# Every fourth MLP weight chunk gets its low part from an accumulating DMA (first half) or from GpSimd (second half)

## The chip, the cores and the metric

One core of a Trainium2 chip runs the kernel in one launch. The metric is the device time of one execution in microseconds (us); lower is better. The engines are PE (TensorE, matmul), ACT (ScalarE), DVE (VectorE), POOL (GpSimd) and SP (SyncE, which here only issues DMAs); each works through its own queue in program order, and semaphores order them among each other. DMAs run on 16 DMA engines beside them.

## The reference

One decoder block on 256 tokens of 2048 features, float32: an mLSTM branch and an attention branch on a shared normalised input, merged by gates, then an MLP with 8192 hidden features and a gated embedding. The change touches the MLP alone:

```python
h = rmsnorm(x, mlp_norm[i])
x = x + jnp.square(jax.nn.relu(h @ w_ff1[i])) @ w_ff2[i]     # 2048 -> 8192 -> 2048
```

## The kernel before

Activations are kept as [feature, token]; a product takes weight tiles of 128 x 128 as the stationary operand and the activation of 256 tokens as the moving one. To get float32 accuracy from a faster pass, each operand is split into a high part H (rounded to float32r) and the exact rest L, and W.a = WH.aH + WH.aL + WL.aH. The activation's two parts lie side by side in one `blk` tile of 512 columns, so each weight tile needs two matmuls: its high part (`wh`) against all 512 columns, and its low part (`wl`) against the first 256.

All weights are packed in the order of their use into 518 chunks of 128 x 1024 (eight weight tiles, 512 KB), and two chunks make a pair, which is one DMA of 1 MB on SP's queue into a staging buffer `wst` (`STAGE` = 3 buffers, line 306). `plan()` lists the groups: after the projections, gates and the output product (226 chunks) come the MLP's 256, in four rounds of four groups `f1` and four groups `f2`, eight chunks each, then the embedding's products `pp` and `pg` (36 chunks). A column tile of f1 or f2 has 16 weight tiles, so every second chunk finishes one.

`run()` walks over the chunks with index i. At each it calls `prep(i + LOOK)`, `LOOK` = 3: ACT casts the staged chunk to `wh` (helper `copy`, line 170). Then the matmuls of chunk i are issued (`mm`, line 210). Then `side()` issues steps of side work (evacuation of finished tiles, splitting of new activations, norms) that a planner with estimated costs finds to fit beside the chunk, and `prep_rest(i + LOOK)`, there or right after: DVE subtracts `wl = wst - wh` (helper `tt`, line 178). `wh` and `wl` have `LOOK + 1` = 4 buffers each. When i + LOOK is odd, `prep_rest` also gives back the staging buffer of that pair and issues the load of the pair three further on (`self.dma(i // 2 + STAGE)`), which has to wait for the readers of the buffer.

A finished column tile of f1 is taken out of PSUM by ACT (`lo<-acc`, half of it) and DVE (`z<-acc,lo`), scaled, squared and split again into a `blk` tile, an operand of f2. A finished tile of f2 is added to x by DVE (`g<-g,acc`, twice). `z`, `lo`, `g`, `rb` and `blk` are these tiles' names in the profile; `load_x` (line 336) loads x, and later x again, into `g`.

Of the kernel before, what the change touches and what calls it, by code (L numbers as in the profile page):

```python
"""Hybrid mLSTM / attention block: one launch, activations kept as [feature, token].

Dense products run on the tensor engine as three float32r passes: every float32 operand is
split exactly into a rounded high part H (float32r) and the exact rest L, and
W.a = WH.aH + WH.aL + WL.aH.  The per-token factor of each RMS norm is applied to the product
instead of to its operand, so no product waits for the statistics.
"""
# [31 lines left out]

# columns of the packed per-feature parameters  # L40
C_G1, C_G2, C_G3, C_G4, C_CW, C_CB, C_MN, C_BIF = 0, 16, 32, 48, 64, 96, 104, 112
NCOL = 113
# columns of the constants
K_ID, K_CA, K_CB, K_FR, K_SG, NCON = 0, 128, 384, 768, 769, 770


def plan():
    """Order in which the weight chunks (128 x 1024) are used."""
    g = []
    for n in range(2):  # L50
        g.append(("av", n))
    g += [("mq", 0), ("mk", 0), ("gate", 0), ("mv", 0), ("mv", 1), ("mo", 0), ("mo", 1)]
    for n in range(2):
        g += [("aq", n), ("ak", n)]
    for n in range(4):
        g += [("gm", n), ("um", n)]
    for n in range(4):
        g += [("ga", n), ("ua", n)]
    for n in range(4):
        g.append(("wo", n))  # L60
    for j in range(4):
        g += [("f1", 4 * j + n) for n in range(4)] + [("f2", 4 * j + n) for n in range(4)]
    for n in range(4):
        g += [("pp", n), ("pg", n)]
    return g


def pack_weights(w_in, w_up_m, w_up_a, w_out, w_ff1, w_ff2, w_pg, w_pp):
    def rows(w):
        """Chunks of two k tiles with 512 columns (these weights are the moving operand)."""  # L70
        return w.reshape(-1, 2, 128, 512).transpose(0, 2, 1, 3).reshape(-1, 128, 1024)

    def tiles(w):
        """Chunks of eight 128 x 128 tiles, all k tiles of one column tile after another."""
        t = w.reshape(w.shape[0] // 128, 128, -1, 128).transpose(2, 0, 1, 3)
        return t.reshape(-1, 8, 128, 128).transpose(0, 2, 1, 3).reshape(-1, 128, 1024)

    out = []
    for name, n in plan():
        c = slice(512 * n, 512 * n + 512)  # L80
        if name == "gate":
            w = np.zeros((D, 128), np.float32)
            w[:, 0:4] = w_in[:, OFF["mi"]:OFF["mi"] + 4]
            w[:, 32:36] = w_in[:, OFF["mf"]:OFF["mf"] + 4]
        elif name in OFF:
            o = OFF[name] + 512 * n
            w = w_in[:, o:o + 512]
        elif name == "um":
            w = w_up_m[:, c]
        elif name == "ua":  # L90
            w = w_up_a[:, c]
        elif name == "wo":
            w = w_out[:, c]
        elif name == "f1":
            w = w_ff1[:, c]
        elif name == "f2":
            j, m = divmod(n, 4)
            w = w_ff2[2048 * j:2048 * j + 2048, 512 * m:512 * m + 512]
        elif name == "pg":
            w = w_pg[:, c]  # L100
        else:
            w = w_pp[:, c]
        out.append(rows(w) if name in ("av", "mv") else tiles(w))
    a = np.concatenate(out)
    return np.ascontiguousarray(a.reshape(-1, 2, 128, 1024).transpose(0, 2, 1, 3))


class Block:
# [21 lines left out]

# [1 line left out]
    @staticmethod  # L132
# [82 lines left out]

# [1 line left out]
    def spawn(self, gen, front=False):  # L217
# [16 lines left out]
    def side(self):  # L234
        """Runs the steps that fit beside the current chunk on the scalar and vector engines."""
        while True:
            lim = self.t["pe"] + BEYOND
            can = [t for t in self.tasks if t[1] <= self.now and t[2] <= lim]
            base = min(self.t["act"], self.t["dve"])
            best = min(can, key=lambda t: max(t[2], base)) if can else None  # L240
            if self.rest:
                r = max(self.t["dve"], self.ready(self.rest[2]))
                if not best or max(best[2], self.t["dve"]) >= r - 0.3:
                    self.prep_rest(self.now + LOOK)
                    continue
            if not best or max(self.t["act"], self.t["dve"]) >= lim:
                return
            self.advance(best)
# [14 lines left out]
    def settle(self, *aps):  # L263
        """Until products that read these would not hold up the tensor engine."""
        while self.ready(*aps) > self.t["pe"] and not self.forcing:
            yield 1
# [7 lines left out]
    def enter(self, kind, limit=2):  # L274
        """At most `limit` heads at a time, as many as there are buffers."""
        while self.inside.get(kind, 0) >= limit:
            yield 1
        self.inside[kind] = self.inside.get(kind, 0) + 1
# [6 lines left out]

# [1 line left out]
    def split(self, blk, src, gain=None):  # L287
        """blk = [H | L] of src (times a per-feature gain)."""
        if gain is None:
# [9 lines left out]
    def dma(self, p, load=True):  # L299
        """Loads two chunks."""  # L300
        if 2 * p >= self.nchunk:
# [6 lines left out]
    def load_w(self, p, a, b):  # L308
        """Part of a pair: its columns a to b."""
        t = self.stage[p].rearrange("p c n -> p (c n)")  # L310
        src = self.d["w"][p].rearrange("p c n -> p (c n)")
        self.nc.sync.dma_start(out=t[:, a:b], in_=src[:, a:b])  # L312

    def prep(self, i, parts=1):
# [8 lines left out]
        if parts == 1:  # L323
            self.copy(h, s)

    def prep_rest(self, i):
        if self.rest:
            l, s, h = self.rest
            self.tt(l, s, h.bitcast(F32), OP.subtract)
            self.rest = None  # L330
# [7 lines left out]
    def warm_up(self):  # L338
        """Keeps the tensor engine busy until the first operands are there, for its clock."""
        t = self.ps.tile([128, 512], F32, name="acc")  # L340
# [5 lines left out]

# [1 line left out]
    def square_in(self, key, src, keep=False):  # L348
# [13 lines left out]
    def rsqrt(self, y, v):  # L362
        """y = v ** -0.5, refined once; [128, few] columns."""
        s = self.tp.tile(list(v.shape), F32, name="rs_s")
# [6 lines left out]
    def spread(self, col):  # L371
        """out[p, t] = col[t] for every p: ones.T @ diag(col)."""
        rd = self.tp.tile([128, 2, 128], F32, name="rd", bufs=2)
# [44 lines left out]

# [1 line left out]
    def gather(self, dst, ps):  # L420
# [56 lines left out]

# [1 line left out]
    def col(self, c):  # L479
# [8 lines left out]
    def halves(self, blk, src, gain=None):  # L488
        """split(), with a step between the two parts."""
        if gain is None:  # L490
# [28 lines left out]
    def tables(self):  # L519
        """cos and signed sin of position * frequency, on the partitions of the rotated features."""  # L520
        yield 5
# [127 lines left out]
    def memory(self, h):  # L649
        """Head h of the mLSTM, in its quadratic form."""  # L650
        yield from self.wait("mv0" if h < 2 else "mv1")
# [52 lines left out]
    def read_out(self):  # L704
        """Normaliser and head norm of all heads, then the gated output."""
        yield from self.wait(*[f"mem{h}" for h in range(MH)])
# [34 lines left out]
    def attend(self, h):  # L741
        """Causal softmax attention of head h (the sequence is one block)."""
        n, m = divmod(h, 4)
# [85 lines left out]

# [1 line left out]
    def operand(self, name, n):  # L831
# [7 lines left out]
    @staticmethod  # L839
    def narrow(name, n):  # L840
        """Whether all three passes add up in the same columns, for a shorter way out."""
        return name == "pp" or (name, n) == ("pg", 3)

    def units(self, name, c):
        """(column tile, k tile) of each part of chunk c of a group."""
        if name in ("av", "mv"):
# [6 lines left out]
    def run(self):  # L853
# [3 lines left out]
        for name, n in groups:  # L857
            c = {"gate": 2, "um": 4, "ua": 4, "pp": 1}.get(name, 8)
            chunks += [(name, n, i, c) for i in range(c)]
        self.nchunk = len(chunks)  # L860
        assert self.nchunk == 2 * d["w"].shape[0]
        self.stage, self.w, self.val, self.acc, self.rb, self.rcol = {}, {}, {}, {}, {}, {}
# [108 lines left out]
    def finish(self):  # L971
        """The final norm."""
        self.forcing = True
# [61 lines left out]
```

## Time and profile before

| | us |
|---|---|
| median of 2 runs | 1502.16 (1501.99 to 1502.33) |
| profiled execution, first to last instruction (span) | 1499.9 |
| PE busy | 1484.6 |
| PE's weight loads busy (beside matmuls) | 1300.2 |
| DVE busy | 1041.5 |
| ACT busy | 760.2 |
| POOL busy | 0.2 |

The profile is of one execution; its times are from the start of the span. Busy times of different engines overlap. PE's matmuls are pipelined and their ends are modelled, so the starts of matmuls tell the pace. "PEld" is the loading of the stationary operand. "<-" in a row of an instruction has the tile written before it and the tiles read behind it.

### The profile page before, as it was taken

The numbers are of one execution on the slowest core, as the hardware profiler recorded it, in microseconds if no ns is written. First come the engines' busy times: TensorE is split into PE (matmuls) and PEld (weight loads), VectorE is DVE, ScalarE is ACT, GpSimd is POOL, SyncE is SP. The second block draws the span as 40 slices with busy tenths as digits, with TensorE's granted clock in tenths as the row PEclk, the third lists the DMA queues.
The fourth block names the chain that finished last, engine by engine and source line by source line (L and its number), as shares of the span: only waits on it lengthen the run. The fifth ranks groups of instructions, "written<-read, shape, count | busy, mean of one in ns | idle before, by whom it ended". The sixth has DMA issues, their size and how long they took to land.

```text
span 1499.9 us, 21023 instructions
## 1 busy us (share of the span) xinstructions
PE 1484.6 (99%) x8500; PEld 1300.2 (87%) x8500; DVE 1041.5 (69%) x1606; ACT 760.2 (51%) x1105; POOL 0.2 (0%) x4
## 2 busy tenths in 40 slices
PE   9999999999999999999999999999999999999996
PEld 7888888888888888888888888888888888888886
DVE  7685568987667677777765677666766567777775
ACT  7565544475445555455443445334543345455663
POOL 0000000000000000000000000000000000000000
PEclk9999999999999999999999999999999999999998
DMA  8554354544545555555555555555555545555451
GB/s 315 195 188 157 141 197 169 197 143 166 196 176 204 207 189 209 191 177 193 182 189 192 195 184 184 195 196 186 182 202 195 196 174 193 197 196 184 182 194 59
DMA packets 41472, 279.97 MB, mean 187 GB/s; under 512 B 4736, under 2 KB 5536, under 8 KB 8608
## 3 DMA queue, kind: packets, MB, share of 16 engines
q1 hardware_dynamic: 41232, 278.58, 51.6%
q8 instruction: 66, 1.08, 0.3%
q14 instruction: 30, 0.25, 0.0%
q10 hardware_dynamic: 144, 0.06, 0.0%
HBM read 276.52 MB, written 2.10 MB: 186 GB/s over the span
## 4 chain that ended last, share of the span: by engine, by line
PE 99%; DVE 0%; DMA 0%; ACT 0%; SPq 0%; issue 0%; DVEq 0%
PE acc L210 98%; DMA wst<-w 0%; DVE g L178 0%; PE acc L214 0%; ACT L811 0%; SPq L336 0%; ACT wh L170 0%; DVE rd L178 0%; DVE z L178 0%; ACT sq L166 0%; SPq L312 0%; ACT z L166 0%; DVEq L1030 0%; ACT rs_s L166 0%; DVE r L205 0%
## 5 line engine op out<-in xcount | busy, mean ns | idle before, releaser
L210 PE MATMUL acc<-blk,wh 128*128 128x512 f32 (+1 forms) x3984 | 1362.4, 389 | 0.0
L210 PE MATMUL acc<-blk,wl 128*128 128x256 f32 x3888 | 1088.5, 280 | 0.0
L210 PEld LDWEIGHTS acc<-blk,wh 128*128 128x128 f32 x3984 | 740.4, 188 | 162.5
L178 DVE TENSOR_TENSOR wl<-wst,wh 128x1024 fp32r<-128x1024 f32 (+1 forms) x521 | 633.6, 1217 | 230.1 <-ACT wh L170 216.8
L170 ACT CAST wh<-wst 128x1024 fp32r<-128x1024 f32 (+1 forms) x521 | 545.4, 1047 | 374.1 <-PE acc L210 316.9
L210 PEld LDWEIGHTS acc<-blk,wl 128*128 128x128 f32 x3888 | 734.4, 189 | 0.4
L170 ACT COPY lo<-acc 128x256 f32<-128x256 f32 x173 | 64.6, 373 | 242.8 <-PE acc L210 242.8
L178 DVE TENSOR_TENSOR g<-g,acc 128x256 f32<-128x256 f32 (+2 forms) x166 | 72.1, 437 | 49.2 <-PE acc L210 46.5
L178 DVE TENSOR_TENSOR z<-acc,lo 128x256 f32<-128x256 f32 x76 | 32.3, 425 | 65.9 <-ACT lo L170 65.9
L178 DVE TENSOR_TENSOR g<-acc,lo 128x256 f32<-128x256 f32 x96 | 40.4, 421 | 46.4 <-ACT lo L170 46.2
L210 PE MATMUL acc<-wh,blk 128*128 128x512 f32 x256 | 70.9, 393 | 1.6 <-ACT wh L170 1.6
L210 PEld LDWEIGHTS acc<-wh,blk 128*128 128x128 f32 x256 | 47.3, 188 | 12.1 <-ACT wh L170 2.6
L210 PE MATMUL acc<-wl,blk 128*128 128x512 f32 x128 | 40.9, 390 | 0.0
L170 ACT CAST blk<-z 128x256 fp32r<-128x256 f32 x64 | 26.1, 408 | 29.1 <-DVE z L189 29.1
L178 DVE TENSOR_TENSOR z<-z,rb 128x256 f32<-128x256 f32 x76 | 32.3, 425 | 3.1 <-ACT rb L170 0.6
L166 ACT ACTIVATE sq<-g 128x256 f32<-128x256 f32 x64 | 25.7, 409 | 10.1 <-DVE g L178 9.5
L210 PEld LDWEIGHTS acc<-wl,blk 128*128 128x128 f32 x128 | 24.0, 188 | 5.5 <-DVE wl L178 0.4
L189 DVE SCALAR_TENSOR_TENSOR z<-z 128x256 f32<-128x256 f32 x64 | 27.2, 424 | 2.2
L178 DVE TENSOR_TENSOR nacc<-nacc,sq 128x256 f32<-128x256 f32 x59 | 24.8, 421 | 3.8 <-ACT sq L166 2.9
L178 DVE TENSOR_TENSOR blk<-z,blk 128x256 fp32r<-128x256 f32 x64 | 26.8, 418 | 0.0
L166 ACT ACTIVATE blk<-g,cols 128x256 fp32r<-128x256 f32 x48 | 23.9, 509 | 2.5 <-DMA cols<-cols 1.4
L178 DVE TENSOR_TENSOR g<-g,rb 128x256 f32<-128x256 f32 (+1 forms) x46 | 24.2, 528 | 1.3
(115 smaller groups left out, 360.0 us busy)
## 6 DMA issues: line engine op xcount, KB each, us to landing
wst<-w SPq DMA_DIRECT2D x256, 1024.0 KB, 4.8
wst<-w SPq DMA_DIRECT2D x4, 512.0 KB, 6.8
g<-x SPq DMA_DIRECT2D x4, 512.0 KB, 5.8
g<-x SPq DMA_DIRECT2D x6, 256.0 KB, 6.9
out_dram<-g SPq DMA_DIRECT2D x3, 512.0 KB, 2.8
wst<-w SPq DMA_DIRECT2D x4, 256.0 KB, 5.6
g<-x SPq DMA_DIRECT2D x4, 128.0 KB, 5.2
con<-con SPq DMA_DIRECT2D x1, 385.0 KB, 8.2
```

The source lines that it names most:

```text
L166: self.nc.scalar.activation(out, in_, func, **kw)
L170: self.nc.scalar.copy(out, in_)
L178: self.nc.vector.tensor_tensor(out, a, b, op=op)
L189: self.nc.vector.scalar_tensor_tensor(out, a, s, b, op0, op1)
L210: self.nc.tensor.matmul(out, lhsT=lhsT, rhs=rhs, start=start, stop=stop)
```

## The change

Of the MLP's 256 chunks those with i % 4 == 1 get their low part in another way; all others as before.

- First half (the first 128 chunks of the MLP): after the cast to `wh`, ACT writes -1 times the staged chunk, rounded to float32r, into `wl`; a DMA issued by POOL then adds the chunk from DRAM, where it lies in float32, into `wl`. The weight is read from DRAM a second time for this.
- Second half: POOL does the subtraction that DVE did.

The helpers that charge the planner are not called for the DMA and for POOL's subtraction; for ACT's copy they are. The rest of the diff takes out comments and docstrings (left out here).

```diff
@@ def prep(self, i, parts=1):
         if parts == 1:
             self.copy(h, s)
+            if self.way(i) == "dma":
+                self.act(l, s, AF.Copy, scale=-1.0)
+
+    def way(self, i):
+        j = i - self.first["f1"]
+        if i % 4 != 1 or not 0 <= j < 256:
+            return "dve"
+        return "dma" if j < 128 else "pool"
 
     def prep_rest(self, i):
         if self.rest:
             l, s, h = self.rest
-            self.tt(l, s, h.bitcast(F32), OP.subtract)
+            way = self.way(i)
+            if way == "dma":
+                self.nc.gpsimd.dma_start(out=l, in_=self.d["w"][i // 2][:, i % 2], accum_op=OP.add)
+            elif way == "pool":
+                self.nc.gpsimd.tensor_tensor(l, s, h.bitcast(F32), op=OP.subtract)
+            else:
+                self.tt(l, s, h.bitcast(F32), OP.subtract)
             self.rest = None
             if i % 2:
                 del self.stage[i // 2]
                 self.dma(i // 2 + STAGE)
@@ def run(self):
+        self.first = {}
+        for i, (name, n, c, nch) in enumerate(chunks):
+            self.first.setdefault(name, i)
```

## Rows read from the trace of the kernel before

**Rows 1.** Page: busy us (share of span) and instructions of each engine.

```profile
PE 1484.6 (99%) x8500; PEld 1300.2 (87%) x8500; DVE 1041.5 (69%) x1606; ACT 760.2 (51%) x1105; POOL 0.2 (0%) x4
```

**Rows 2.** Page: chain that ended last, share of the span by engine.

```profile
PE 99%; DVE 0%; DMA 0%; ACT 0%; SPq 0%; issue 0%; DVEq 0%
```

**Rows 3.** PE's waits, whole span: us in total, times, longest us.

```profile
PE acc L210 <- ACT sq L166: 2.4, 1, 2.4
PE acc L210 <- DVE rd L178: 1.7, 1, 1.7
```

**Rows 4.** Stretches: us, busy us (instructions) by engine, granted clock, DMA share, GB/s.

```profile
673.00:1027.00 354.00, 354.00 (x2045) 312.13 (x2044) 232.69 (x326) 157.07 (x194) 0.00 (x0) 1.00 0.53 189
1027.00:1381.00 354.00, 354.00 (x2045) 312.14 (x2044) 243.35 (x352) 168.16 (x224) 0.00 (x0) 1.00 0.53 190
```

**Rows 5.** Tiles wl and wh, 673:1381: duration ns min/median/max, first and last start.

```profile
L210 PEld LDWEIGHTS acc<-blk,wl x2040: 187/189/192, 673.1 to 1380.9; 128*128 128x128 f32 x186
L178 DVE TENSOR_TENSOR wl<-wst,wh x256: 1216/1226/1226, 672.2 to 1380.4; 128x1024 fp32r<-128x1024 f32 x128
...
L170 ACT CAST wh<-wst x255: 1048/1053/1056, 673.9 to 1379.3; 128x1024 fp32r<-128x1024 f32 x128
```

**Rows 6.** Timeline of PE: start us, us, line, what; three chunks begin in it.

```profile
760.73 0.39 PE L210 MATMUL acc<-blk,wh 128*128 128x512 f32 x1
760.96 0.28 PE L210 MATMUL acc<-blk,wl 128*128 128x256 f32 x1
761.08 0.39 PE L210 MATMUL acc<-blk,wh 128*128 128x512 f32 x1
...
763.50 0.39 PE L210 MATMUL acc<-blk,wh 128*128 128x512 f32 x1
...
766.28 0.39 PE L210 MATMUL acc<-blk,wh 128*128 128x512 f32 x1
```

**Rows 7.** Timeline of ACT, DVE and SP there; in brackets idle before, and its releaser.

```profile
760.93 0.37 ACT L170 COPY lo<-acc 128x256 f32<-128x256 f32 x1 [1.80 <-PE acc L210]
761.20 1.05 ACT L170 CAST wh<-wst 128x1024 fp32r<-128x1024 f32 x1
762.60 1.22 DVE L178 TENSOR_TENSOR wl<-wst,wh 128x1024 fp32r<-128x1024 f32 x1
762.72 0.41 ACT L170 CAST blk<-z 128x256 fp32r<-128x256 f32 x1 [0.46 <-DVE z L189]
763.85 10.73 SPq L306 DMA_DIRECT2D wst<-w  x3
766.36 1.05 ACT L170 CAST wh<-wst 128x1024 fp32r<-128x1024 f32 x1 [1.68 <-PE acc L210]
```

**Rows 8.** Page: DMA issues with KB each and median us from issue to landing.

```profile
wst<-w SPq DMA_DIRECT2D x256, 1024.0 KB, 4.8
...
g<-x SPq DMA_DIRECT2D x4, 512.0 KB, 5.8
...
out_dram<-g SPq DMA_DIRECT2D x3, 512.0 KB, 2.8
```

**Rows 9.** Tile wst, whole span: landing of its loads.

```profile
DMA to landing us min/median/max: 4.2/4.8/8.9
```

**Rows 10.** Stretches of one weight load, issued at 763.85; last columns DMA share, GB/s.

```profile
763.85:764.80 0.95, 0.95 (x8) 0.83 (x7) 0.39 (x2) 0.83 (x1) 0.00 (x0) 1.00 0.00 0
764.80:765.80 1.00, 1.00 (x7) 0.89 (x6) 1.00 (x1) 0.00 (x0) 0.00 (x0) 1.00 0.60 164
765.80:766.80 1.00, 1.00 (x7) 0.90 (x6) 0.46 (x2) 0.44 (x1) 0.00 (x0) 1.00 0.98 418
766.80:767.80 1.00, 1.00 (x7) 0.88 (x7) 0.87 (x3) 0.61 (x1) 0.00 (x0) 1.00 1.00 426
767.80:768.70 0.90, 0.90 (x7) 0.78 (x6) 0.87 (x1) 0.00 (x0) 0.00 (x0) 1.00 0.12 46
```

**Rows 11.** Timeline of POOL, one of its four instructions.

```profile
0.30 0.10 POOL L1025 MEMSET const-bfloat16-1.0<- 128x1 bf16 x1
```

## The prediction

> **What bounds the kernel now.** I read the page's busy line and chain first, then PE's waits, then the two halves of the MLP as stretches of their own, and last a timeline of a few chunks. The busy line and the chain say the same: PE is busy 99% of the span and the chain that ends last is PE for 99% [rows 1, 2]. The longest of PE's four kinds of named waits are 2.4 and 1.7 us in the whole span [rows 3]. A busy PE need not be a PE at its peak, so I look at the pace: in the MLP the matmuls start in a fixed rhythm, one pair (512 columns with the high part, 256 with the low part) every 0.35 us, one chunk of eight pairs every 2.77 us (763.50 - 760.73; 766.28 is again 2.78 on) [rows 6]. The MLP takes from about 673 to 1381 us, 256 x 2.77 = 709 us, and PE is busy in 354.00 of 354.00 us of each half, at a granted clock of 1.00, the 2.4 GHz level [rows 4]. There is no wait in this stretch for the change to remove. DVE (66% and 69% there) and ACT (44% and 48%) both have room, POOL has done nothing, and the DMA engines are 53% busy [rows 4].
>
> So the question is only whether the new way of making the low part is ready when PE wants it.
>
> **The window.** Chunk i+3 is prepared while PE works on chunk i. Of the four buffers for low parts the one it takes was read last by chunk i-1, so the work starts when chunk i-1 ends and must be done when chunk i+3 starts: three chunks, 8.3 us, whatever happened earlier. No lead can be built up, so a part that is late is late anew each time. In an f1 stretch ACT first copies the finished column tile (760.93), then casts the high part (761.20, 1.05 us) [rows 7]. The chunk began at 760.73, so chunk i+3 begins at 760.73 + 3 x 2.77 = 769.04; its first matmul with the low part starts 0.23 later, as 760.96 after 760.73 [rows 6], and the weight load ahead of that takes 0.19 [rows 5]: the low part is wanted at 769.08. In f2 there is no copy before the cast: chunk start 766.28, cast 766.36, wanted at 774.63 [rows 6, 7]. Today DVE's subtraction is done by 763.82 in the first case (762.60 + 1.22), five microseconds early.
>
> **The change, part by part.**
>
> *Chunks.* f1 and f2 hold 256 chunks and begin at chunk 226; those with i % 4 == 1 are 64, 32 in each half. Of the first 32, half are prepared behind an f1 chunk and half behind an f2 chunk.
>
> *Removed:* 64 subtractions on DVE at 1.226 us [rows 5], 78 us of busy time, all of it hidden under PE. Worth 0.
>
> *Added on ACT, first half:* 32 copies of 128x1024 scaled by -1. The nearest row is the cast of the same shape, 1.05 us [rows 5]; 34 us more on an engine that is busy 157 of 354 us [rows 4]. They stand right behind the cast on ACT. Queued behind is the cast of the hidden tile (762.72 in the f1 example [rows 7]), which would start at about 763.3; its user is an f2 chunk, at the earliest one and a half chunks on. 0 by itself, but it delays the start of the DMA.
>
> *Added on POOL, first half:* 32 accumulating DMAs of 512 KB, issued when ACT's copy is done: 761.20 + 2 x 1.05 = 763.30 in f1, 766.36 + 2.10 = 768.46 in f2. Window to landing: 769.08 - 763.30 = 5.8 us, and 774.63 - 768.46 = 6.2 us. PE's first weight load of a low part waits for it, all matmuls behind it in order, and ACT's next cast behind those: each late microsecond goes to the end of the kernel in full.
>
> How long does such a DMA take? The trace has none. From below: 512 KB out of the core at the end, with the engines free, land in 2.8 us [rows 8]; then it is hidden. The nearest row in size and surroundings is the four loads of 512 KB of x, made beside the stream of weights: 5.8 us [rows 8]. Beside a weight load this one stands as well, and by more than chance: i is odd in every such chunk, so the same line of the program that issues it then issues the load of the next pair, which waits for the same ACT copy (the last reader of the staging buffer). SP's load has no traffic for 0.95 us after its issue at 763.85, and then fills the 16 engines, 0.98 to 1.00 busy at 418 to 426 GB/s, for two of the four microseconds that it takes [rows 10]. Both want the same engines in the same microseconds. An addition into memory has also to fetch the old values: another 512 KB, at 426 GB/s 1.23 us. POOL has to write the descriptors, which SP's queue does not need; for that I put 0.3 us, a third of SP's own 0.95. Sum: 5.8 + 1.23 + 0.3 = 7.3 us. From above: the slowest of all weight loads, in the crowd at the start, landed after 8.9 us [rows 9], with 0.3 for POOL 9.2.
>
> The nearest row decides, with the second fetch. Late by 7.3 - 5.8 = 1.5 us behind f1 and 7.3 - 6.2 = 1.1 us behind f2: 16 x 1.5 + 16 x 1.1 = 41.6 us. At 9.2 us it is 16 x 3.4 + 16 x 3.0 = 102 us, at 2.8 us nothing.
>
> Without the second fetch the DMA would land after 6.1 us, 0.3 us late in f1 only, 5 us in all. The Trainium skill, "Collectives: The Full Stack", section "The bandwidth ceiling: the fold count and why AG ≠ RS ≠ AR", bears on this: it says that an adding transfer is slower not by the addition but by its two source reads, which share one read ring, so that it runs at half the rate of a copy. No run here shows it yet; with it the sum is 41.6 us, without it 5 us.
>
> *Added on POOL, second half:* 32 subtractions of 128x1024. POOL's only rows are one-column memsets of 0.10 us [rows 11], of no use. From below DVE's 1.226 us. From above there is the window: the high part is there at 762.25 in f1, wanted at 769.08, so anything under 6.8 us, five and a half times DVE's time, costs PE nothing. I take 0. What hides it is the three-chunk window; if POOL needed 8 us it would be 1.2 us each, 38 us in all.
>
> *Moved:* the next pair's load follows ACT or POOL instead of DVE. Now it is issued 3.1 us into the chunk (763.85 - 760.73 [rows 6, 7, 10]), lands 4.8 us later [rows 8] at 7.9, and is wanted five chunks after the chunk's start, at 13.9: 6 us to spare, enough for the 1.2 to 2.5 us that sharing engines with the accumulating DMA may take or for a POOL that is slower than DVE. 0. Traffic: 16.8 MB more to read from memory and as much to fetch in the core, in 354 us; the stretch moves 189 GB/s, 67 MB, at 53% [rows 4], so 0.53 x (1 + 33.6 / 67) = 0.80 at most on average: the engines don't become the bound. The planner no longer charges DVE for these subtractions and may place side steps earlier; DVE has a third of its time free. 0.
>
> **Sum:** span 1499.9 + 41.6 = 1541.5 us, and 2.3 us around it (1502.16 median of the runs less 1499.9): **1544 us**, 2.8% slower.
>
> **The rivals.**
>
> *The DMA is hidden, or nearly* (not slower): it lands within 6.9 us, at most 0.9 us late on the mean window of 6.0. Then 0 to 30 us, 1502 to 1532 us. The point from which it decides is a landing at 5.8 to 6.2 us. For it: 512 KB alone in 2.8 us, and the x loads at just 5.8. Against it: twice the bytes to read and a weight load released in the same moment. Chance 0.38.
>
> *The DMA is very late:* over 9.2 us, because the engines add slowly or POOL needs microseconds to write its descriptors. At 12 us it would be 16 x 6.2 + 16 x 5.8 = 192 us, 1694 us. No row speaks for it, none excludes it. Chance 0.15.
>
> *POOL and DVE hold each other off in the second half.* DVE is busy 243 of 354 us [rows 4], 7.6 us in four chunks of 11.1; less one subtraction 6.4, leaving 4.7 us. If DVE stood still whenever POOL reads, a POOL subtraction of over 4.7 us would make DVE the bound; at 6 us, 1.3 us in each of 32, 42 us, with the DMA hidden 1544 us as well but lost in the other half. Chance 0.03. The Trainium skill, "SBUF — State Buffer", section "Who interferes with whom", says that a DVE instruction with two SBUF inputs is blocked by a GpSimd instruction that reads SBUF; and "GPSIMD Engine Reference", section "Elementwise — side-by-side cycle accounting", gives 4497 ns for 2048 columns on GpSimd, by which I estimate 2.25 us here, well under that point. No row shows POOL's price yet.
>
> *Faster by over 2%:* would need 30 us out of a stretch in which PE never waits. Chance 0.01.
>
> **How the numbers follow.** My forecast, a landing between 6.9 and 9.2 us and so a loss of 30 to 102 us (1532 to 1604 us), gets 0.43; the others as above. 2% is 30 us, about what a measurement of this kernel can tell from no change. Faster 0.01; within 2% 0.38; slower 0.43 + 0.15 + 0.03 = 0.61. The range takes in the hidden case and my own up to 9.2 us: 1500 to 1604 us, leaving out the very late one and the odd ones. My forecast's own range is 1532 to 1604.
>
> **What would show each step.** Right: PE waits, about 32 of them, for a DMA into wl between 673 and about 1070 us, 1 to 2 us each, and none behind it; a DMA row wl<-w of 32 issues with a median near 7.3 us; an ACT row of 32 scaled copies near 1.05 us; a POOL row of 32 subtractions under 6.8 us; PE's pace of 2.77 us for a chunk unchanged between the waits. Wrong: a landing under 6 us and no waits (hidden), a POOL queue that issues much later than ACT's copy ends, PE waits for POOL or DVE in the second half, or a PE pace that differs without waits, for which nothing in the trace of before prepares me.

## The result and the profile after

| | before | after |
|---|---|---|
| median of the runs, us | 1502.16 | 1576.43 (1573.18 to 1579.68, 2 runs) |
| profiled execution, span, us | 1499.9 | 1577.9 |

The changed kernel is slower: ratio 1.0495, 95% interval 1.0444 to 1.0547. The prediction was 1544 us, 2.8% slower, with a range to 1604; the sign and the place were right, the size was 74 us instead of 42.

The page's engine line and the chain that ended last, of the changed kernel, answer [rows 1, 2]:

```profile
PE 1509.9 (96%) x8500; PEld 1305.8 (83%) x8500; DVE 1008.4 (64%) x1542; ACT 788.4 (50%) x1137; POOL 108.1 (7%) x68
...
PE 80%; DMA 16%; ACT 1%; DVE 1%; issue 0%; SPq 0%; DVEq 0%; ACTq 0%
```

A chain that was PE for 99% now passes through a DMA for 16%. PE's waits in the whole span (us in total, times, longest us), against [rows 3], name it:

```profile
PE acc L210 <- DMA wl<-w: 53.5, 32, 2.1
```

and the weight loads' own:

```profile
PEld acc L210 <- DMA wl<-w: 63.8, 32, 2.4
```

All 32 accumulating DMAs are late, by about 2 us, and nothing else is new: no wait for POOL's 32 subtractions. The instructions that write wl (duration ns min/median/max, first and last start), against [rows 5]:

```profile
L166 ACT ACTIVATE wl<-wst x32: 1048/1058/1065, 672.1 to 1086.2; 128x1024 fp32r<-128x1024 f32 x32
L340 POOL DMA_DIRECT2D wl<-w x32: 862/862/1016, 673.5 to 1087.6; - x32
L342 POOL TENSOR_TENSOR wl<-wst,wh x32: 2391/2506/2619, 1099.4 to 1449.9; 128x1024 fp32r<-128x1024 f32 x32
```

The loss by halves is read from ACT's casts into `wh`, one for each chunk. The MLP's first starts at 671.13 us before and at 671.14 after. These are the casts 128 and 256 chunks later, before:

```profile
1027.05 1.06 ACT L170 CAST wh<-wst 128x1024 fp32r<-128x1024 f32 x1 [1.72 <-PE acc L210]
1382.09 1.06 ACT L170 CAST wh<-wst 128x1024 fp32r<-128x1024 f32 x1 [1.74 <-PE acc L210]
```

and after:

```profile
1098.23 1.05 ACT L170 CAST wh<-wst 128x1024 fp32r<-128x1024 f32 x1 [3.49 <-PE acc L210]
1460.04 1.05 ACT L170 CAST wh<-wst 128x1024 fp32r<-128x1024 f32 x1 [1.78 <-PE acc L210]
```

The first half took 427.1 us for 355.9, 71.2 more; the second 361.8 for 355.0, 6.8 more. Together 78, the difference of the spans.

The second half has no new wait. It is slower because PE's pace is: in a stretch of 100 us of the changed kernel (columns as in [rows 4]) there are 568 matmuls, 284 pairs, of 0.353 us; 579 in the same stretch of e2 below, 0.3467 us as before.

```profile
1100.00:1200.00 100.00, 100.00 (x568) 86.67 (x567) 72.15 (x93) 47.69 (x68) 22.64 (x9) 1.00 0.53 188
```

The DMA table's new row beside [rows 8], KB each and median us to landing (SP's loads of 1 MB stay at 4.8):

```profile
wl<-w POOLq DMA_DIRECT2D x32, 512.0 KB, 7.9
```

One of the 32, in order of time. First the issue: ACT, SP and POOL in the timeline; SP's load and POOL's DMA both wait for ACT's copy, which ends at 766.68.

```profile
765.62 1.06 ACT L166 ACTIVATE wl<-wst 128x1024 fp32r<-128x1024 f32 x1
766.58 0.39 ACT L170 CAST blk<-z 128x256 fp32r<-128x256 f32 x1
766.70 0.33 SPq L306 DMA_DIRECT2D wst<-w  x1
766.97 0.86 POOL L340 DMA_DIRECT2D wl<-w  x1 [12.63 <-ACT blk L170]
```

Then the DMA engines from POOL's issue on (last two columns: their share, GB/s). Up to 771.37 they move 246 to 295 GB/s, which is SP's load of 1 MB: 0.42 + 0.59 MB in the two long stretches. Only then comes a stretch in which they are full (1.03) and yet move 201 GB/s, with PE busy half of it: the addition, 4.4 us after its issue.

```profile
766.97:767.67 0.70, 0.70 (x7) 0.62 (x6) 0.43 (x1) 0.57 (x2) 0.70 (x1) 1.00 0.12 12
767.67:769.37 1.70, 1.70 (x12) 1.50 (x11) 1.19 (x1) 0.48 (x1) 0.17 (x1) 1.00 0.83 246
769.37:771.37 2.00, 2.00 (x14) 1.75 (x13) 0.98 (x4) 1.32 (x2) 0.00 (x0) 1.00 0.87 295
771.37:774.47 3.10, 1.54 (x9) 1.10 (x7) 2.54 (x4) 1.45 (x2) 0.00 (x0) 1.00 1.03 201
```

And PE: the matmul with the low part starts 2.27 us after the one ahead of it instead of 0.23, and what follows runs at half the clock for a while.

```profile
772.52 0.39 PE L210 MATMUL acc<-blk,wh 128*128 128x512 f32 x1
774.79 0.38 PE L210 MATMUL acc<-blk,wl 128*128 128x256 f32 x1 [1.88 <-DMA wl<-w]
775.01 0.55 PE L210 MATMUL acc<-blk,wh 128*128 128x512 f32 x1
...
776.22 0.63 PE L210 MATMUL acc<-blk,wh 128*128 128x512 f32 x1
776.64 0.41 PE L210 MATMUL acc<-blk,wl 128*128 128x256 f32 x1
```

The granted clock of that stretch is 0.50, the 1.2 GHz level, after a wait of 2 us:

```profile
775.10:778.50 3.40, 3.40 (x12) 2.88 (x11) 0.00 (x0) 0.00 (x0) 0.00 (x0) 0.50 0.54 227
```

So three things are to be explained: why each DMA lands after 7.9 us, what the falls of the clock add, and why PE keeps a slower pace where it waits for nothing.

### The profile page after: what moved, and what is told of

Same layout as the page of the kernel before. It is cut to its first block, busy times and chain, and to the rows that moved or that the text cites. A ratio compares the mean times of both kernels' runs of the same rounds, so it can differ in the third digit from the quotient of the medians.

```text
span 1577.9 us, 21147 instructions
## 1 busy us (share of the span) xinstructions
PE 1509.9 (96%) x8500; PEld 1305.8 (83%) x8500; DVE 1008.4 (64%) x1542; ACT 788.4 (50%) x1137; POOL 108.1 (7%) x68
## 4 chain that ended last, share of the span: by engine, by line
PE 80%; DMA 16%; ACT 1%; DVE 1%; issue 0%; SPq 0%; DVEq 0%; ACTq 0%
PE acc L210 80%; DMA wl<-w 16%; DVE g L178 1%; ACT wl L166 1%; DMA wst<-w 0%; PE acc L214 0%; ACT wh L170 0%; ACT L826 0%; SPq L351 0%; DVE rd L178 0%; DVE z L178 0%; ACT sq L166 0%; SPq L312 0%; ACT z L166 0%; DVEq L1048 0%
## 5 line engine op out<-in xcount | busy, mean ns | idle before, releaser
L210 PE MATMUL acc<-blk,wh 128*128 128x512 f32 (+1 forms) x3984 | 1379.2, 393 | 0.0
L210 PEld LDWEIGHTS acc<-blk,wl 128*128 128x128 f32 x3888 | 736.5, 189 | 64.2 <-DMA wl<-w 63.8
L178 DVE TENSOR_TENSOR wl<-wst,wh 128x1024 fp32r<-128x1024 f32 (+1 forms) x457 | 554.9, 1215 | 249.1 <-ACT wh L170 239.4
L340 POOL DMA_DIRECT2D wl<-w x32 | 27.8, 868 | 1060.2 <-ACT wl L166 855.5
L342 POOL TENSOR_TENSOR wl<-wst,wh 128x1024 fp32r<-128x1024 f32 x32 | 80.2, 2505 | 283.7 <-ACT wh L170 283.7
L178 DVE TENSOR_TENSOR blk<-z,blk 128x256 fp32r<-128x256 f32 x64 | 53.4, 834 | 21.3 <-ACT blk L170 21.3
L189 DVE SCALAR_TENSOR_TENSOR blk<-g,cols,blk 128x256 fp32r<-128x256 f32 x48 | 35.3, 743 | 9.1 <-ACT blk L166 9.1
L166 ACT ACTIVATE wl<-wst 128x1024 fp32r<-128x1024 f32 x32 | 33.8, 1057 | 0.0
```

The costliest lines, as they stand in the source:

```text
L166: self.nc.scalar.activation(out, in_, func, **kw)
L178: self.nc.vector.tensor_tensor(out, a, b, op=op)
L189: self.nc.vector.scalar_tensor_tensor(out, a, s, b, op0, op1)
L210: self.nc.tensor.matmul(out, lhsT=lhsT, rhs=rhs, start=start, stop=stop)
L340: self.nc.gpsimd.dma_start(out=l, in_=self.d["w"][i // 2][:, i % 2], accum_op=OP.add)
L342: self.nc.gpsimd.tensor_tensor(l, s, h.bitcast(F32), op=OP.subtract)
```

## The experiments

The theories on the DMA: **A**, its data queue behind SP's load, which the same ACT copy releases and which is issued 0.27 us ahead; **B**, the start by POOL takes 4.4 us by itself. On the pace: **1**, it is a state that a break in PE's sequence can set and that lasts until the next; **2**, POOL's work slows PE. In all kernels with the DMA alone (e1, e3 to e6, e9) the second half is done by DVE as before; each of these six was run once. Runs of the kernel before beside them lie between 1501.3 and 1502.4 us.

**e1: the accumulating DMAs alone.**

```diff
-        return "dma" if j < 128 else "pool"
+        return "dma" if j < 128 else "dve"
```

> Only the accumulating DMAs of the first half; the second half is done by DVE as before. In the changed kernel the first half cost 71.2 us and the second 6.8 us, the latter without any wait, as a slower pace of PE (284 pairs of matmuls in 100 us where there were 289 or 290). Theory 1 (the pace is a state that PE falls into after a stall and keeps): second half again some 7 us slower, 1576 us in all. Theory 2 (POOL's work slows PE): second half as before, 1571 us. Both: 32 waits for the DMA, 59 us.

Measured 1587.3 us (one run; span 1585.5). The second half is slow without POOL, 284 pairs in 100 us:

```profile
1200.00:1300.00 100.00, 100.00 (x569) 86.67 (x568) 60.15 (x77) 38.72 (x41) 0.00 (x0) 1.00 0.53 192
```

Theory 2 falls. The total is 11 us above what I expected: 32 waits again, of 66.9 us on PE's weight loads, and a mean clock of 0.988 where the changed kernel had 0.993. This run had seven falls of the clock after waits, the changed kernel's profiled one three. In each of these 3.4 us a pair takes some 0.64 us instead of 0.35, so about 1.5 us are lost, and four more make 6. The waits are 3.1 us longer (66.9 for 63.8), and the pace between them is some 2 us better than in the changed kernel. Together that is about the 7.6 between the two spans.

**e2: POOL's subtractions alone.**

```diff
-        return "dma" if j < 128 else "pool"
+        return "dve" if j < 128 else "pool"
```

> Only the subtractions on POOL in the second half; the first half as before. Theory 1 (pace is a state after a stall): no stalls, pace stays at 289 to 290 pairs in 100 us, 1502 us. Theory 2 (POOL's work slows PE): 284 pairs in 100 us in the second half, 1509 us. Rival from the prediction (POOL and DVE hold each other off): PE waits for wl from DVE or POOL.

Measured 1501.95 us, ratio 1.0001 (0.9992 to 1.0011). The pace is the quick one, with POOL at work:

```profile
1100.00:1200.00 100.00, 100.00 (x579) 88.15 (x578) 57.59 (x75) 41.41 (x46) 22.12 (x9) 1.00 0.53 196
```

POOL's half of the change costs nothing. DVE and POOL do hold each other off, though: DVE's subtraction that splits the hidden activations, 418 ns in every case before, now takes up to five times that (second half, ns min/median/max):

```profile
L178 DVE TENSOR_TENSOR blk<-z,blk x32: 416/1248/2093, 1035.3 to 1295.4; 128x256 fp32r<-128x256 f32 x32
```

It is hidden, as the prediction's rival had it for a POOL subtraction under 4.7 us; it takes 2.5.

**e3: the load of the next pair placed one chunk later in the program.**

```diff
             if i % 2:
                 del self.stage[i // 2]
-                self.dma(i // 2 + STAGE)
+                if way == "dma":
+                    self.owed = i // 2 + STAGE
+                else:
+                    self.dma(i // 2 + STAGE)
+            elif self.owed is not None:
+                self.dma(self.owed)
+                self.owed = None
```

> As e1_dma_only, but SP's load of the next pair is issued one chunk (2.8 us) later, so that the accumulating DMA no longer has it in front. In the changed kernel the first data of the DMA came 4.4 us after POOL's issue, just when the load's data ended. Theory A (the DMA queues behind the load): first data after some 1.5 us, landing after about 5 us, hardly a stall, 1502 to 1510 us. Theory B (the start by software takes 4.4 us by itself): first data again after 4.4 us, landing after 7.9 us or later, 59 us or more of waits, 1570 to 1580 us.

Measured 1574.7 us, but the edit did not do what it was to do. SP has nothing else in its queue, so its load waits for the staging buffer alone and goes at the same moment wherever it stands in the program, 0.26 us ahead of POOL again:

```profile
766.85 0.33 SPq L307 DMA_DIRECT2D wst<-w  x1
767.11 0.86 POOL L341 DMA_DIRECT2D wl<-w  x1 [12.53 <-ACT blk L171]
```

It says nothing on A and B. It does say something on the pace: with the same 32 waits, the second half ran at the quick pace this time.

```profile
1100.00:1200.00 100.00, 100.00 (x579) 88.15 (x578) 70.24 (x105) 48.94 (x69) 0.00 (x0) 1.00 0.53 191
```

**e4: the same DMA without the addition.** The low part then holds the whole weight.

```diff
-                self.nc.gpsimd.dma_start(out=l, in_=self.d["w"][i // 2][:, i % 2], accum_op=OP.add)
+                self.nc.gpsimd.dma_start(out=l, in_=self.d["w"][i // 2][:, i % 2])
```

> As e1_dma_only, but the DMA overwrites instead of adding, so the low part holds the whole weight: the addition is left out. If the second fetch of the addition is what makes a packet of 4 KB take 328 ns, it falls to about half, the data to 1.5 us from 3.1, landing to 6.3 us, stalls to 0.3 us each, 10 us in all: 1510 to 1520 us. If the packets are slow because POOL's queue or the change of type makes them so: 328 ns again, landing 7.9 us, 1570 us or more.

Measured 1515.1 us. Landing 5.8 us, and of POOL's queue (packets, MB, share of 16 engines) this run's share, against the changed kernel's:

```profile
q0 software_dynamic: 4608, 16.78, 3.0%
...
wl<-w POOLq DMA_DIRECT2D x32, 512.0 KB, 5.8
```

```profile
q0 software_dynamic: 4608, 16.78, 5.4%
```

3.0% of 1513.3 us is 1.42 us of all 16 engines for each DMA, 5.4% of 1577.9 us is 2.66: the addition costs 1.24 us of the engines, as a second fetch of the same size would. PE's weight loads wait for it 8 times, 2.5 us in all, and only one such wait (1.0 us) is long enough to hold up matmuls by more than a few tenths. The kernel is still 13 us slower than before, some 11 of it pace: 0.353 us a pair through most of the MLP (quick again from about 917 to 1008 us), which over all its 2048 pairs would be 2048 x 0.0067 = 13.7 us.

```profile
1100.00:1200.00 100.00, 100.00 (x567) 86.73 (x567) 62.58 (x84) 40.88 (x48) 0.00 (x0) 1.00 0.53 191
```

**e9: the load of the next pair really later.** A copy of one column on DVE, behind the next chunk's subtraction, reads the staging buffer last; SP has to wait for it.

```diff
+            elif self.owed is not None:
+                old, p = self.owed
+                self.owed = None
+                self.tcopy(self.mark, old[:, 1, 0:1])
+                self.dma(p)
```

> As e1_dma_only, but SP's load of the next pair waits for a one-column copy on DVE behind the next chunk's subtraction (a later reader of the staging buffer), so it is issued about 3 us after POOL's DMA and its data can't be in front. e3_late_load had only moved it in the program: SP issued it 0.27 us ahead of POOL again, so it told nothing. Theory A (the DMA queues behind the load): first data some 1.5 to 2.5 us after POOL's issue instead of 4.4, landing after 5 to 6 us, no waits, 1502 to 1516 us by PE's pace. Theory B (the start takes 4.4 us by itself): first data after 4.4 us, then shared with the load, landing after 8 to 10 us, waits of 60 us or more, 1575 to 1640 us.

Measured 1512.1 us: theory A. POOL now issues 2.9 us ahead of SP,

```profile
807.82 0.86 POOL L342 DMA_DIRECT2D wl<-w  x1 [10.23 <-ACT wl L168]
810.47 0.15 DVE L176 COPY mark<-wst 128x1 f32<-128x1 f32 x1
810.68 0.33 SPq L308 DMA_DIRECT2D wst<-w  x1
```

the engines are idle for 1.5 us and full with the addition right after,

```profile
807.82:809.32 1.50, 1.50 (x11) 1.34 (x10) 0.00 (x0) 1.05 (x1) 0.86 (x1) 1.00 0.00 0
809.32:810.32 1.00, 1.00 (x8) 0.88 (x7) 1.00 (x1) 0.00 (x0) 0.00 (x0) 1.00 1.11 74
```

and it lands after 5.5 us (min/median/max):

```profile
DMA to landing us min/median/max: 5.4/5.5/6.0
```

So POOL's start is some 1.6 us, and 2.8 of the 4.4 were queueing. The 10 us that are left are pace: 579 matmuls in 100 us at first, 568 later. PE's weight load waited for one of these DMAs once, for 0.3 us at 891.6, the only such wait that the profile names. It is not what made PE slow: by the starts of the matmuls the slow pace begins at 880.3, ends at this wait, and begins again at 902.9. What stands at those two places is shown behind e11.

```profile
740.00:840.00 100.00, 100.00 (x579) 88.15 (x578) 53.04 (x83) 49.80 (x56) 7.76 (x9) 1.00 0.76 239
900.00:1000.00 100.00, 100.00 (x568) 86.86 (x567) 53.69 (x86) 51.29 (x61) 7.77 (x9) 1.00 0.75 236
...
PEld acc L212 <- DMA wl<-w: 0.3, 1, 0.3
```

**e5: ACT's copy for the low part ahead of its cast.**

```diff
+            if self.way(i) == "dma":
+                self.act(l, s, AF.Copy, scale=-1.0)
             self.copy(h, s)
-            if self.way(i) == "dma":
-                self.act(l, s, AF.Copy, scale=-1.0)
```

> As e1_dma_only, but ACT writes -1 times the chunk before it casts the high part, so POOL can issue 1.05 us earlier, and SP's load, which waits for the cast, comes after POOL's issue. Theory B (a fixed start): landing 7.9 us after the issue as before, each of 32 waits 1.05 us shorter, about 0.8 instead of 1.85 us, 26 us in all: 1530 to 1545 us with the pace and the clock. Theory A: the DMA is ahead of the load, first data well before 4.4 us, no waits, 1502 to 1516 us.

Measured 1544.1 us, the time that theory B gave and not A's. But the fixed start of B is not there. POOL issues 0.67 us ahead of SP here, and the engines are idle for 1.5 us and then busy, as in e9:

```profile
810.19:811.69 1.50, 1.50 (x10) 1.29 (x10) 0.00 (x0) 0.84 (x2) 0.86 (x1) 1.00 0.00 0
811.69:814.20 2.51, 2.51 (x17) 2.22 (x16) 1.23 (x1) 0.86 (x1) 0.00 (x0) 1.00 0.88 137
```

It still lands late: the load shares the engines with it, and the landing, 8.0 us in the median, is no better than behind the load. So of the 32 waits only what POOL gains in time of issue comes off, and of that some two thirds:

```profile
PE acc L210 <- DMA wl<-w: 30.9, 32, 1.6
```

Theory A was too narrow: the accumulating DMA loses whether the load is ahead of it or beside it. With waits of about 1 us no fall of the clock shows: the run's mean is 0.996, as before.

**e6: only the second half of the columns by DMA.** DVE subtracts the first half, ACT copies 512 columns.

```diff
-                self.act(l, s, AF.Copy, scale=-1.0)
+                self.act(l[:, 512:], s[:, 512:], AF.Copy, scale=-1.0)
...
-                self.nc.gpsimd.dma_start(out=l, in_=self.d["w"][i // 2][:, i % 2], accum_op=OP.add)
+                self.nc.gpsimd.dma_start(out=l[:, 512:], in_=self.d["w"][i // 2][:, i % 2, 512:],
+                                         accum_op=OP.add)
+                self.tt(l[:, :512], s[:, :512], h[:, :512].bitcast(F32), OP.subtract)
```

> As e1_dma_only, but only columns 512 to 1023 of the low part come by the accumulating DMA (256 KB); DVE subtracts the others. The first matmul that wants the DMA's columns is then the fifth of eight, 1.39 us later; ACT's copy is some 0.45 us shorter and the data half. If the lateness of 1.85 us is what costs, it is gone: no waits, 1502 us at the quick pace, 1515 us if PE falls into the slow one. If waits stay, something else than the time to landing makes them.

Measured 1502.5 us. The DMA lands after 6.8 us, behind the load as ever, and PE does not wait: it is lateness against the window that costs, not the DMA.

**e8 and e12: breaks in PE's sequence, in the kernel before.** A matmul of one column whose result is not used, ahead of every sixteenth chunk from 98 to 210 (e8), or ahead of each of the six chunks 290 to 295 (e12). No DMA on POOL, no wait.

```diff
             self.prep(i + LOOK)
+            if 98 <= i < 226 and i % 16 == 2:       # e12: if 290 <= i < 296:
+                self.mm(self.new_bank()[:, 0:1], self.ones, self.ones[:, 0:1])
```

> The kernel before with one matmul of 128x1 (float32, own PSUM bank, result unused) ahead of every sixteenth chunk from chunk 98 to 210: eight small breaks in PE's sequence. Theory (the pace is a state that a break may set anew and that stays until the next): between breaks some stretches run at 0.347 us for a pair, others at 0.353 us, constant within a stretch, and the time moves by up to 8 us either way plus 2 us for the eight: 1494 to 1510 us. If the pace belongs to what the phase computes, all stretches from 290 to 670 us stay at 0.353: 1504 us.

> The kernel before with one matmul of 128x1 (float32, result unused) ahead of each of chunks 290 to 295, in the MLP; no DMA on POOL, no wait for anything. Theory (a small break can leave PE in the slow pace until the next): pairs at 0.353 instead of 0.347 us from there to the end of the MLP in some or all runs, up to 10 us slower, 1504 to 1514 us, runs in two groups. If only waits for DMA do it: 0.347 us throughout, 1503 us.

e8: 1503.15 us, ratio 1.0008 (0.9999 to 1.0018): no gain and hardly a loss. Yet the pace did change. Before the MLP the kernel before is slow without a change from 360 us on. In e8's profile it is quick from one of the eight breaks (535.66) to the next (580.27), as between two earlier ones, and slow again behind. The same stretch in e8 and before:

```profile
540.00:572.00 32.00, 32.00 (x187) 28.00 (x186) 23.33 (x35) 16.74 (x27) 0.00 (x0) 1.00 0.56 210
540.00:572.00 32.00, 32.00 (x183) 27.72 (x182) 22.90 (x34) 16.56 (x26) 0.00 (x0) 1.00 0.57 209
```

So a break can set the quick pace as well as the slow one; three of the eight (444.8, 490.2, 625.7) changed nothing. e12: 1513.5 us, ratio 1.0076 (1.0061 to 1.0091), in all four runs 1512.7 to 1513.8. Its pace ahead of the six matmuls, and behind them to the end of the MLP:

```profile
740.00:840.00 100.00, 100.00 (x579) 88.19 (x578) 63.12 (x84) 41.62 (x46) 0.00 (x0) 1.00 0.52 192
900.00:1000.00 100.00, 100.00 (x569) 86.68 (x568) 64.11 (x88) 42.62 (x52) 0.00 (x0) 1.00 0.52 190
```

Six matmuls of one column cost 11.5 us, 10 of them because the 1500 pairs behind them in the MLP take 0.0067 us more each. Theory 1 is shown: a small break is enough, without a DMA and at a granted clock of 1.00. The kernel before has the slow pace too, in the stretch ahead of the MLP, where I had not counted it (545 in 96 us, 568 in 100):

```profile
560.00:656.00 96.00, 96.00 (x545) 83.23 (x544) 68.87 (x105) 49.07 (x72) 0.00 (x0) 1.00 0.54 192
```

**e10 and e11: the whole change, repaired in either way,** with POOL's half: e10 holds the load back as e9, e11 sends half the columns by DMA as e6.

> The whole change, with the load of the next pair held back behind DVE in the first half as in e9_load_after_dve. Theory (all the loss is the DMA's queueing behind the load and what the waits bring with them in clock and pace): landing 5.5 us, no waits of a microsecond, 1502 us where PE keeps the quick pace, up to 1516 us where a tiny wait throws it into the slow one; single runs anywhere between. Rival (the two halves hurt each other, or POOL has a price of its own): over 1516 us.

> The whole change, with only columns 512 to 1023 by the accumulating DMA as in e6_half, POOL in the second half. Theory: lead instead of lateness, no wait, pace undisturbed: 1502 us, the same as before within 0.3%. Nothing can make it faster than before, since PE is the bound in both halves.

e10: median 1511.1 us, single runs from 1503.3 to 1515.0, ratio 1.0058 (1.0037 to 1.0079): from the fastest, the profiled one, which is slow in the MLP only from 924.4 to 1014.7 us, to ones in which PE may have lost the quick pace early. e11: median 1502.0, ratio 1.0014 (0.9997 to 1.0032), seven runs at 1501.4 to 1502.9 and three at 1510.7 to 1511.5. One of the three is the profiled one, and it is the pace again: 567 matmuls in 100 us from 1000 us on, without a named wait for a DMA.

The trace shows where it began. As a rule a weight load and the matmul ahead of it start together (the first two rows). At 903.4, just as the DMA that POOL issued at 896.02 lands, a weight load of a low part starts 0.03 us behind (the last two). No matmul is held up, but from here on the pace is the slow one.

```profile
903.03 0.39 PE L210 MATMUL acc<-blk,wh 128*128 128x512 f32 x1
903.03 0.19 PEld L210 LDWEIGHTS acc<-blk,wl 128*128 128x128 f32 x1
...
903.38 0.39 PE L210 MATMUL acc<-blk,wh 128*128 128x512 f32 x1
903.41 0.19 PEld L210 LDWEIGHTS acc<-blk,wl 128*128 128x128 f32 x1
```

The same stands at both falls of the pace in e9 (880.31 and 902.93, 0.05 and 0.04 us behind) and at both changes in e10, to slow at 924.35 (0.11) and to quick at 1014.73 (0.05). Four other late starts in these runs and e6, of 0.03 to 0.22 us, changed nothing. That the late start sets the pace is read from these places alone; no run tried it. Neither kernel is faster than before, as it had to be with PE the bound.

## Why the prediction was right, and where it was short

*The window and the mechanism:* right. PE waits 32 times in the first half for a DMA into wl, nothing in the second half, and each late microsecond reaches the end.

*ACT's copy and POOL's subtraction:* the copy takes 1.06 us (1.05 assumed); POOL's subtraction 2.5 us, inside the window, with no effect in e2. The rival in which DVE and POOL hold each other off happens, up to 2093 ns for 418 in e2, and costs nothing. What the Trainium skill says in "SBUF — State Buffer", section "Who interferes with whom", on a DVE instruction with two SBUF inputs beside a GpSimd instruction that reads SBUF, agrees with that row.

*The landing:* 7.9 us for 7.3. Of the three terms the second, 1.23 us for the second fetch, is 1.24 by the engines' shares in the changed kernel and e4. The rule on two source reads that the Trainium skill has in "Collectives: The Full Stack", section "The bandwidth ceiling: the fold count and why AG ≠ RS ≠ AR", agrees (2.66 us against 1.42, a ratio of 1.9). The first, 5.8 us from the loads of x, has the size of e4's landing, but that is luck: e4's DMA too is issued by POOL, behind a load, so its 5.8 us hold POOL's start and a wait in the queue. The third, 0.3 us for POOL, was too small: with the engines idle the first data come 1.6 us after POOL's issue (e9) and 0.95 after SP's [rows 10], 0.6 us more. From e4 to the changed kernel the landing grows by 2.1 us (7.9 - 5.8). Of that 1.24 are engine time and 0.33 POOL's longer issue (0.86 against 0.53); the rest stays open. Besides, POOL issues 0.29 us after ACT's copy has ended, where I had nothing. That the sum was near does not mean that its picture was: I had the DMA and the load share the engines, while the data wait for 2.8 us behind the load and then have the engines to themselves. e5 shows that sharing comes to the same.

*The size:* the waits, taken as what is over 0.23 us between the two matmuls at each, make 59 us, 1.84 each; I had 1.3. That is 17 of the 36 us that the spans' difference of 78 is above the 41.6 forecast. The other 19 are the step that failed: "PE's pace of 2.77 us for a chunk unchanged between the waits". The falls of the clock took 3 x 1.5, some 5 us, and the slow pace 6.8 us in the second half. The rest of the first half's 71 us is 7 (71 - 59 - 5): some 3 because the matmul behind each late one starts 0.22 us after it (775.01 less 774.79) instead of 0.12 [rows 6], and some 4 of pace, which changed from wait to wait there. For the falls of the clock I had no term at all. I had written that nothing in the trace of before prepares for a pace that differs without waits. That was wrong: the trace has both paces, and the stretch at 560 to 656 us shows it.

*The rivals:* hidden, very late and a bound on DVE did not come. The second is not far in kind: e9 shows that the price hangs on a neighbouring load, released by the same ACT instruction.

## What to carry to other kernels

Where the bound is PE and a part has a fixed window, price a new producer by the time to landing with its neighbours, and ask which other DMA the same semaphore releases: here the DMA needs 5.5 us alone and 7.9 behind a load that had 6 us to spare. A load can't be delayed by moving it in the program when its queue is empty; it needs something to wait for. And where PE runs without a break at a quick pace, count a break not by its length alone: look at the pace of the stretches on both sides of it. A part that is ready with no time to spare is not free either: e9, and e11 in three of ten runs, lost 9 to 10 us with next to no wait.

## What the runs showed of the hardware that I had not expected

- PE has two paces for the same sequence of matmuls, 0.3467 and 0.3534 us a pair, at a granted clock of 1.00. Which one it has after a break is not told by the break's cause: the second half was slow in e1 and quick in e3, after 32 waits in both. It can last for hundreds of microseconds. Five changes in e9, e10 and e11 came at a weight load that started 0.03 to 0.11 us late, with no matmul held up. Why there are two was not tried.
- A DMA issued by POOL 0.27 us after a load of 1 MB from SP had its first data 4.4 us after its issue, when the load's were through; alone, after some 1.6 us.
- After a wait of about 2 us the granted clock fell to 0.50 for 3.4 us in some cases, three of 32 in the changed kernel and e3 and seven of 32 in e1, and in none of 32 in e5 with waits of about 1 us.
